# Linear attention on one core: one subtraction over both halves of a level's exponents, and an exponential for each half

## The chip, the cores and the metric

The kernel runs on one core of a Trainium2 chip. The metric is the device time in microseconds (us) of one execution. The core has five engines that run beside each other, each through its own list of instructions in order: PE (TensorE, matrix products), DVE (VectorE), ACT (ScalarE), POOL (GpSimd) and SP (SyncE, which issues most transfers). They wait for one another by semaphores.

## The reference, cut to what matters

The program is one inference step of a hybrid encoder. The part that is changed is gated linear attention, branch C: four heads, keys and values of 96 channels, with a decay that differs by channel and step.

```
def step(S, inp):
    qc, kc, vc, ac = inp
    b = jnp.cumsum(ac, axis=1)
    o_inter = jnp.einsum('blhk,bhkv->blhv', qc * jnp.exp(b), S)
    rel = b[:, :, None] - b[:, None, :]
    decay = jnp.exp(jnp.where(causal, rel, -jnp.inf))
    att = jnp.einsum('bthk,bshk,btshk->bhts', qc, kc, decay)
    o_intra = jnp.einsum('bhts,bshv->bthv', att, vc)
    bL = b[:, -1]
    S_new = jnp.exp(bL)[..., None] * S + jnp.einsum('bshk,bshv->bhkv', kc * jnp.exp(bL[:, None] - b), vc)
    return S_new, o_inter + o_intra
```

There are 512 prompt tokens and 8 x 16 sample tokens. Around this stand the input projections, stick-breaking attention (branch A), a pooling mixer (branch B), the gates and projections of the three branches, cross-attention and a feed-forward layer.

## The kernel before, in words

Tokens are worked in five tiles of 128: four of the prompt (0 to 3) and one of the samples (4), in the order 0, 1, 4, 2, 3. `gla_prep(i)` makes, for a tile, the transposed queries and keys (`qT`, `kT`), the log decays `la` (L721) and their running sums `bT` (matmul `pb`, L725, then ACT copies it, L728), and `E`, `kd` and `eL`. `gla_main(i)` computes the 128x128 attention of each head by levels of halving: at a level `hh` (64, 32, 16, 8, 4, 2, 1; for samples 8, 4, 2, 1) the tile is cut into blocks of 2*hh tokens, and the queries of a block's second half meet the keys of its first half. Both are scaled by the exponential of their distance from a reference, the running sum at the last token of the first half. `X`, a tile of 96x512 with two buffers, holds the scaled keys in each block's first half and the scaled queries in its second half. Four matmuls `pl` (L779) multiply them, and a predicated copy (L782) puts the result into `attT`.

So a level of hh > 1 is a chain over the engines: two subtractions on DVE (L771, L772), one exponential on ACT (L773), two products on DVE (L774 with the keys, L775 with the queries), `pl` on PE, the copy on DVE. There are 27 such levels (4 x 6 + 3), and five of hh = 1, which subtract only for the queries (L767, L768). The row forms in the trace tell the level: `pl` is 64, 96, 112, 120, 124, 126 or 127 rows high for hh = 64 to 1.

No order is written out by hand in this stage. A scheduler lists each engine's instructions when the program is built, and takes what is later in the program when what is earlier isn't ready by its own estimate. So PE's list here weaves the small matmuls of linear attention with the big ones of `branch` A, which comes next in the program: units of 24 matmuls `ps_g` (a gate) and 9 matmuls `ps_b` (a projection), each 128x320. This text calls them fill. A unit's gate is read by ACT (L875, the first of three exponential and logarithm steps with L877, L878; DVE clamps between, L876), and its projection by DVE (L883, into `mrg`). `ps_g` and `ps_b` share two PSUM buffers (tag "g"), so the next `ps_g` can start only when an earlier `ps_g` was read at L875 or an earlier `ps_b` at L883. The four units of the first 256 columns carry the weights `ga0` and `ba` in their names, the last four `ga3`.

Of the kernel before, what the change touches and what calls it, by code (L numbers as in the profile page):

```python
# [12 lines left out]
AF = mybir.ActivationFunctionType  # L13
ALU = mybir.AluOpType
# [14 lines left out]
TAU = 16.0  # L29
# [4 lines left out]
def tile_hybrid_stream_step(  # L34
# [9 lines left out]
    nc = tc.nc  # L44
# [18 lines left out]
    def bank(shape, tag="z", name="ps"):  # L63
        bufs = {"g": 2, "t": 2, "z": 2, "o": 2}[tag]
        return psum.tile(shape, F32, tag=tag, bufs=bufs, name=name)
# [243 lines left out]
    for hh in (64, 32, 16, 8, 4, 2, 1):  # L309
        nb = 64 // hh  # L310
# [433 lines left out]
    def gla_main(i, pre, S):  # L744
# [12 lines left out]
        for hh in levels:  # L757
            nb = 64 // hh
            nk = P - hh
            X = glw.tile([96, 4, P], F32, tag="X", bufs=2, name="X")  # L760

            def vw(t):
                return t.rearrange("p h (n two c) -> p (h n) two c", two=2, c=hh)
            bv, xv, kv, qv = vw(bT), vw(X), vw(kT), vw(qT)
            ref = bv[:, :, 0, hh - 1:hh].broadcast_to([96, 4 * nb, hh])
            if hh == 1:
                nc.vector.tensor_tensor(xv[:, :, 1, :], bv[:, :, 1, :], ref, ALU.subtract)  # L767
                nc.scalar.activation(xv[:, :, 1, :], xv[:, :, 1, :], AF.Exp, scale=1.0 / TAU)  # L768
                nc.gpsimd.tensor_copy(xv[:, :, 0, :], kv[:, :, 0, :])
            else:  # L770
                nc.vector.tensor_tensor(xv[:, :, 0, :], ref, bv[:, :, 0, :], ALU.subtract)  # L771
                nc.vector.tensor_tensor(xv[:, :, 1, :], bv[:, :, 1, :], ref, ALU.subtract)  # L772
                nc.scalar.activation(X, X, AF.Exp, scale=1.0 / TAU)  # L773
                nc.vector.tensor_tensor(xv[:, :, 0, :], xv[:, :, 0, :], kv[:, :, 0, :], ALU.mult)  # L774
            nc.vector.tensor_tensor(xv[:, :, 1, :], xv[:, :, 1, :], qv[:, :, 1, :], ALU.mult)  # L775
            pl = bank([P, 4, nb, hh], "z", "pl")
            for h in range(4):
                mv_ = X[:, h, :].rearrange("p (n two c) -> p n two c", two=2, c=hh)[:, :, 1, :]
                nc.tensor.matmul(pl[0:nk, h], X[:, h, 0:nk], mv_, start=True, stop=True)  # L779
            av = attT.rearrange("p h (n two c) -> p h n two c", two=2, c=hh)[0:nk, :, :, 1, :]  # L780
            mk = lmask[hh][0:nk, None, :, None].broadcast_to([nk, 4, nb, hh]).bitcast(U32)
            nc.vector.copy_predicated(av, mk, pl[0:nk])  # L782
# [71 lines left out]
    for j, i in enumerate(order):  # L854
        nxt = gla_prep(order[j + 1]) if j + 1 < NT else None
        if i == 4:
            gla_main(i, pre, None)
        else:
            S = gla_main(i, pre, S)
        pre = nxt  # L860
# [51 lines left out]
    X = resid.tile([P, NT, D], F32, name="X")  # L912
# [687 lines left out]
```

## Time and profile before

| what | value |
|---|---|
| time, median of 3 runs | 1289.25 us (1288.69 to 1289.4) |
| time of the profiled execution | 1288.69 us |
| its span, first to last instruction | 1287.0 us |
| outside the span | 1.69 us |
| mean granted TensorE clock | 0.995 |
| busy: PE, DVE, ACT, POOL | 1254.8, 778.7, 592.1, 43.3 us |

Busy time is the sum of an engine's instructions. What is left of the span for PE, 32.2 us, is the time in which it had nothing to run.

### The profile page before, as it was taken

How to read it: one execution, taken by the hardware profiler on the slowest of the kernel's cores; microseconds unless marked ns; L12 is line 12 of the kernel's file. 1: busy time of each engine (PE TensorE's matmuls, PEld its weight loads, DVE VectorE, ACT ScalarE, POOL GpSimd, SP SyncE). 2: the span in 40 equal slices, each digit the busy share in tenths (PEclk: the TensorE clock that was granted, in tenths of full speed). 3: DMA queues.
4: the chain of work that ended last, by engine and by line, in shares of the span. 5: the costliest groups of instructions: out<-in, count | busy, mean ns of one | idle time of the engine just before them, and what ended most of it. 6: DMA issues, size and time to landing. Idle time of an engine off the chain costs nothing.

```text
span 1287.0 us, 21345 instructions
## 1 busy us (share of the span) xinstructions
PE 1254.8 (98%) x8493; PEld 1151.8 (89%) x8493; DVE 778.7 (61%) x1456; ACT 592.1 (46%) x1200; POOL 43.3 (3%) x162
## 2 busy tenths in 40 slices
PE   8998989999999999999999999999999999999997
PEld 8997768988999999987998888889898989899996
DVE  7332767487478555537535544598466767675667
ACT  5323666555353445435444443475352525243353
POOL 2100121001000000000000000000000000000000
PEclk9999999999999999999999999999999999999999
DMA  7324232101321232231348960243132313132233
GB/s 241 102 79 132 86 100 62 53 15 56 83 65 46 83 96 72 95 131 66 121 160 299 324 227 1 82 148 95 54 107 72 100 50 114 50 99 83 83 109 121
DMA packets 132889, 133.88 MB, mean 104 GB/s; under 512 B 15798, under 2 KB 116741, under 8 KB 132789
## 3 DMA queue, kind: packets, MB, share of 16 engines
q1 hardware_dynamic: 132501, 132.23, 32.8%
q8 instruction: 67, 1.10, 0.4%
q0 software_dynamic: 288, 0.29, 0.1%
q14 instruction: 33, 0.27, 0.1%
HBM read 121.72 MB, written 10.77 MB: 103 GB/s over the span
## 4 chain that ended last, share of the span: by engine, by line
PE 88%; DVE 5%; ACT 2%; issue 2%; DMA 2%; POOL 0%; SPq 0%; DVEq 0%; ACTq 0%; POOLq 0%
PE ps_g L114 13%; PE fX L1351 11%; PE ps_d L114 8%; PE fZ L1351 5%; PE ps_n L114 5%; PE ps_b L114 4%; PE ps_xq L114 4%; PE acc L1423 4%; PE acc L1422 4%; PE acc L1424 4%; PE fY L1351 3%; PE ps_qk L114 3%; PE pl L779 2%; PE ps_xv L114 2%; PE ps_xk L114 2%
## 5 line engine op out<-in xcount | busy, mean ns | idle before, releaser
L1422 PE MATMUL acc<-wh_o,ga_h 128*128 128x512 f32 (+1 forms) x224 | 87.3, 390 | 0.0
L1423 PE MATMUL acc<-wl_o,ga_h 128*128 128x512 f32 (+1 forms) x224 | 87.2, 389 | 0.0
L1424 PE MATMUL acc<-wh_o,ga_l 128*128 128x512 f32 (+1 forms) x224 | 87.2, 389 | 0.0
L875 ACT ACTIVATE sgm<-ps_g 128x320 f32<-128x320 f32 x48 | 20.9, 436 | 65.6 <-PE ps_g L114 65.5
L1424 PEld LDWEIGHTS acc<-wh_o,ga_l 128*128 128x128 f32 x224 | 42.0, 188 | 9.6
L1422 PEld LDWEIGHTS acc<-wh_o,ga_h 128*128 128x128 f32 x224 | 42.0, 188 | 9.2
L1423 PEld LDWEIGHTS acc<-wl_o,ga_h 128*128 128x128 f32 x224 | 42.1, 188 | 9.2
L1351 PE MATMUL fX<-fT_h,wl_f 128*128 128x320 f32 x160 | 49.5, 309 | 0.0
L1351 PE MATMUL fX<-fT_l,wh_f 128*128 128x320 f32 x160 | 49.4, 309 | 0.0
L1351 PE MATMUL fZ<-S_h,wl_f 128*128 128x320 f32 x160 | 49.4, 309 | 0.0
L1351 PE MATMUL fX<-fT_h,wh_f 128*128 128x320 f32 x160 | 49.4, 309 | 0.0
L1351 PE MATMUL fX<-S_h,wh_f 128*128 128x320 f32 x160 | 49.4, 309 | 0.0
L1351 PE MATMUL fX<-S_l,wh_f 128*128 128x320 f32 x160 | 49.4, 309 | 0.0
L1351 PE MATMUL fZ<-S_l,wh_f 128*128 128x320 f32 x160 | 49.4, 308 | 0.0
L1351 PE MATMUL fZ<-S_h,wh_f 128*128 128x320 f32 x160 | 49.4, 308 | 0.0
L1351 PE MATMUL fX<-S_h,wl_f 128*128 128x320 f32 x160 | 49.3, 308 | 0.0
L143 ACT CAST wh_f<-ra 128x1024 fp32r<-128x1024 f32 x20 | 21.0, 1052 | 46.3 <-PE acc L1424 27.1
L144 DVE TENSOR_TENSOR wl_f<-ta,wh_f 128x1024 fp32r<-128x1024 f32 x20 | 24.5, 1226 | 27.5 <-ACT wh_f L143 27.5
L876 DVE TENSOR_SCALAR sgm<-sgm 128x320 f32<-128x320 f32 x48 | 15.5, 325 | 40.4 <-ACT sgm L875 40.3
L143 ACT CAST wh_f<-ta 128x1024 fp32r<-128x1024 f32 x20 | 21.0, 1049 | 38.9 <-PE acc L1424 29.0
L144 DVE TENSOR_TENSOR wl_f<-ra,wh_f 128x1024 fp32r<-128x1024 f32 x20 | 24.5, 1223 | 23.8 <-ACT wh_f L143 23.6
L1507 DVE TENSOR_TENSOR X<-acc,X 128x512 f32<-128x512 f32 x40 | 27.2, 690 | 18.1 <-PE acc L1424 18.1
(1001 smaller groups left out, 4218.2 us busy)
## 6 DMA issues: line engine op xcount, KB each, us to landing
raw_o<-in_w_ffn_out_dram SPq DMA_DIRECT2D x22, 512.0 KB, 3.5
ra<-in_w_ffn_in_dram SPq DMA_DIRECT2D x40, 256.0 KB, 3.3
rb<-in_w_ffn_in_dram SPq DMA_DIRECT2D x40, 256.0 KB, 3.3
kc<-in_cache_mem_k_dram SPq DMA_DIRECT2D x16, 512.0 KB, 5.1
vc<-in_cache_mem_v_dram SPq DMA_DIRECT2D x16, 512.0 KB, 5.5
raw_mix<-in_w_mix_out_dram SPq DMA_DIRECT2D x8, 512.0 KB, 4.2
raw_xo<-in_w_xo_dram SPq DMA_DIRECT2D x8, 512.0 KB, 4.6
kn<-in_cache_sb_k_dram SPq DMA_DIRECT2D x24, 128.0 KB, 2.5
```

What stands on the lines that cost most here:

```text
L114: ins = nc.tensor.matmul(ps, a, b, start=(j == 0), stop=(j == len(todo) - 1))
L143: nc.scalar.copy(h, src)
L144: nc.vector.tensor_tensor(l, src, h.bitcast(F32), ALU.subtract)
L779: nc.tensor.matmul(pl[0:nk, h], X[:, h, 0:nk], mv_, start=True, stop=True)
L875: nc.scalar.activation(s, ps, AF.Exp, scale=-1.0)
L876: nc.vector.tensor_scalar(s, s, 2.0 ** 63, None, ALU.min)
L1351: nc.tensor.matmul(ps, w_, m_, start=(start and j == 0), stop=(stop and j == 11), skip_group_check=True)
L1422: nc.tensor.matmul(ps, ah, wh[:, 0, c0:c0 + w], start=first, stop=False)
L1423: nc.tensor.matmul(ps, ah, wl[:, 0, c0:c0 + w], start=False, stop=False)
L1424: nc.tensor.matmul(ps, al, wh[:, 0, c0:c0 + w], start=False, stop=last)
L1507: nc.vector.tensor_tensor(dst, ps, dst, addop)
```

## The change

One subtraction over the whole of `X` takes the reference from both halves, so both halves hold b - ref. The first half needs ref - b, so its sign is wrong, and the exponential is done for each half by itself with the scales -1/TAU and +1/TAU. Nothing else is edited. The lines after L773 move down by one in the changed kernel: L774 and L775 are L775 and L776 there, L779 is L780, L782 is L783, L883 is L884.

```diff
             else:
-                nc.vector.tensor_tensor(xv[:, :, 0, :], ref, bv[:, :, 0, :], ALU.subtract)
-                nc.vector.tensor_tensor(xv[:, :, 1, :], bv[:, :, 1, :], ref, ALU.subtract)
-                nc.scalar.activation(X, X, AF.Exp, scale=1.0 / TAU)
+                both = bv[:, :, 0:1, hh - 1:hh].broadcast_to([96, 4 * nb, 2, hh])
+                nc.vector.tensor_tensor(xv, bv, both, ALU.subtract)
+                for r_ in range(2):
+                    nc.scalar.activation(xv[:, :, r_, :], xv[:, :, r_, :], AF.Exp, scale=(-1.0, 1.0)[r_] / TAU)
                 nc.vector.tensor_tensor(xv[:, :, 0, :], xv[:, :, 0, :], kv[:, :, 0, :], ALU.mult)
             nc.vector.tensor_tensor(xv[:, :, 1, :], xv[:, :, 1, :], qv[:, :, 1, :], ALU.mult)
```

The scheduler lists the instructions of this stage anew. Three places show it.

PE, from the state product `pk` of tile 1 through the levels of the sample tile 4, and the preparation of tile 3 (`pb`, `pd`, `tp_q`, `tp_k`, `tp_lr`). Before:

```order
L822 MATMUL pk<-vg_nat,qk_nat 96x96 x4
L755 MATMUL pa<-qT,kT 128x128
L779 MATMUL pl<-X 120x64 x4
L114 MATMUL ps_b<-oa_h,wl_ba_3844 128x320
L114 MATMUL ps_g<-hT_h,wh_ga0a 128x320
...
L779 MATMUL pl<-X 124x64 x4
L114 MATMUL ps_g<-hT_h,wl_ga0b 128x320
...
L725 MATMUL pb<-tri,la 96x128 x4
```

In the list before, 25 fill matmuls stand between `pk` and `pb`: one and 14 around the first level's end, 10 behind the second. Changed:

```order
L823 MATMUL pk<-vg_nat,qk_nat 96x96 x4
L780 MATMUL pl<-X 120x64 x4
L780 MATMUL pl<-X 124x64 x4
L725 MATMUL pb<-tri,la 96x128 x4
L732 MATMUL pd<-la,suf 128x384
L780 MATMUL pl<-X 126x64 x4
L780 MATMUL pl<-X 127x64 x4
L703 MATMUL tp_q<-ident,qk_nat 96x128 x4
L707 MATMUL tp_k<-ident,qk_nat 96x128 x4
L755 MATMUL pa<-qT,kT 128x128
L711 MATMUL tp_lr<-ident,lr_nat 16x128
```

All fill is gone from between them: those 25, and 13 more that stood between `pb` and the last `pa`. The next `ps_g` comes six rows further down.

DVE at the same place, from the update of the state `S` with `pk` to the log decays `la` that `pb` multiplies, and on to the products into `mrg` that free the fill's buffers. Changed (before, one L883 stood ahead of tile 1's last L782, and the second four rows behind L721):

```order
L829 SCALAR_TENSOR_TENSOR S<-S,eL,pk 96x96 x4
...
L772 TENSOR_TENSOR X<-bT 96x512
...
L845 TENSOR_TENSOR vg_nat<-po_g,t 128x384
L721 SCALAR_TENSOR_TENSOR la<-z_g,la 128x384
L847 TENSOR_TENSOR vg_nat<-vg_nat,qk_nat 128x384
L776 TENSOR_TENSOR X<-X,qT 96x128x2
L776 TENSOR_TENSOR X<-X,qT 96x256
L884 TENSOR_TENSOR mrg<-ps_b,sgm 128x320 x2
```

Two reads of `ps_b`, which before stood apart and earlier, stand together behind the sample tile's last two levels. Both "g" buffers hold a `ps_b` until then.

PE at the last levels of tile 2, changed (before, 14 fill matmuls stood between levels 124 and 126, and 8 between 126 and 127):

```order
L114 MATMUL ps_b<-oa_h,wl_ba_4390 128x320
L780 MATMUL pl<-X 124x64 x4
L899 MATMUL tp_oc<-ident,vg_nat 128x128 x5
L780 MATMUL pl<-X 126x64 x4
L780 MATMUL pl<-X 127x64 x4
L755 MATMUL pa<-qT,kT 128x128 x4
```

Five small transposes (`tp_oc`) are left between level 124 and level 126, and nothing between 126 and 127.

## Rows read from the trace of the kernel before

**Rows 1.** The page, part 1: busy time of each engine.

```profile
PE 1254.8 (98%) x8493; PEld 1151.8 (89%) x8493; DVE 778.7 (61%) x1456; ACT 592.1 (46%) x1200; POOL 43.3 (3%) x162
```

**Rows 2.** Busy time in stretches: engines, then PE clock, DMA share, GB/s.

```profile
core 0: us, PE busy (x) PEld busy (x) DVE busy (x) ACT busy (x) POOL busy (x), PEclk, DMA share, GB/s
240.00:420.00 180.00, 176.09 (x1301) 162.83 (x1300) 125.60 (x328) 86.32 (x178) 8.69 (x25) 1.00 0.19 53
420.00:1280.00 860.00, 856.32 (x5455) 788.66 (x5453) 519.55 (x880) 385.79 (x756) 0.21 (x1) 1.00 0.35 113
```

**Rows 3.** Timeline of PE from 236 to 425 us, its rows with idle time.

```profile
282.64 0.97 PE L779 MATMUL pl<-X 96*112 96x64 f32 x8 [0.57 <-DVE X L775]
289.69 0.42 PE L114 MATMUL ps_b<-oa_h,wh_ba 128*128 128x320 f32 x1 [0.53 <-ACT sgm L875]
368.51 0.65 PE L779 MATMUL pl<-X 96*64 96x64 f32 x8 [0.15 <-DVE X L775]
376.82 0.41 PE L114 MATMUL ps_b<-oa_h,wh_ba 128*128 128x320 f32 x1 [0.53 <-ACT sgm L875]
400.23 0.97 PE L779 MATMUL pl<-X 96*112 96x64 f32 x8 [1.53 <-DVE X L775]
407.75 1.95 PE L779 MATMUL pl<-X 96*126 96x64 f32 x16 [0.39 <-DVE X L775]
```

**Rows 4.** Groups by form: busy us, mean ns, idle ahead and its releaser.

```profile
L771 DVE TENSOR_TENSOR X<-bT 96x256 f32<-96x256 f32 x27 | 11.2, 415 | 1.0 <-PE pk L807 0.5 <-ACT bT L728 0.5
L772 DVE TENSOR_TENSOR X<-bT 96x256 f32<-96x256 f32 x27 | 11.1, 412 | 0.0
L773 ACT ACTIVATE X<-X 96x512 f32<-96x512 f32 x27 | 16.9, 627 | 20.9 <-DVE X L772 20.9
L741 DVE TENSOR_TENSOR E<-E,qT 96x512 f32<-96x512 f32 x5 | 3.4, 683 | 0.8 <-POOL eL L738 0.7
```

**Rows 5.** Timeline of DVE: start, duration, instruction; one after another.

```profile
280.67 0.69 DVE L741 TENSOR_TENSOR E<-E,qT 96x512 f32<-96x512 f32 x1 [0.67 <-POOL eL L738]
281.27 0.55 DVE L735 TENSOR_TENSOR qk_nat<-qk_nat 128x384 f32<-128x384 f32 x1
...
284.65 0.41 DVE L771 TENSOR_TENSOR X<-bT 96x256 f32<-96x256 f32 x1
284.99 0.41 DVE L772 TENSOR_TENSOR X<-bT 96x256 f32<-96x256 f32 x1
```

**Rows 6.** Timeline of ACT, instructions one after another.

```profile
282.86 0.63 ACT L773 ACTIVATE X<-X 96x512 f32<-96x512 f32 x1 [0.48 <-DVE X L772]
283.40 0.51 ACT L835 ACTIVATE qk_nat<-qk_nat 128x384 f32<-128x384 f32 x1
...
290.00 0.45 ACT L768 ACTIVATE X<-X 96x256 f32<-96x256 f32 x1
290.33 0.47 ACT L877 ACTIVATE sgm<-sgm 128x320 f32<-128x320 f32 x1
```

**Rows 7.** Timeline of PE from `pk` of tile 1 to `pb`.

```profile
296.64 0.84 PE L822 MATMUL pk<-vg_nat,qk_nat 128*96 128x96 f32 x8
297.32 0.41 PE L755 MATMUL pa<-qT,kT 96*128 96x128 f32 x2
297.57 0.95 PE L779 MATMUL pl<-X 96*120 96x64 f32 x8
298.33 0.40 PE L114 MATMUL ps_b<-oa_h,wl_ba 128*128 128x320 f32 x1
298.56 0.31 PE L114 MATMUL ps_g<-hT_h,wh_ga0a 128*128 128x320 f32 x1
298.71 0.32 PE L114 MATMUL ps_g<-hT_l,wh_ga0a 128*128 128x320 f32 x1
...
303.05 1.11 PE L725 MATMUL pb<-tri,la 128*96 128x128 f32 x8
```

**Rows 8.** Timeline of DVE over the same stretch.

```profile
297.52 0.98 DVE L828 SCALAR_TENSOR_TENSOR S<-S,eL,pk 96x96 f32<-96x96 f32 x4 [0.37 <-PE pk L822]
298.42 0.54 DVE L842 TENSOR_REDUCE ss<-sq 128x4 f32<-128x384 f32 x1
298.89 0.68 DVE L756 TENSOR_TENSOR attT<-pa,ident 128x512 f32<-128x512 f32 x1
...
299.96 0.42 DVE L782 COPY_PREDICATED attT<-lm,pl 120x256 f32<-120x256 uint32 x1
300.29 0.15 DVE L160 TENSOR_TENSOR t<-t,m 128x4 f32<-128x4 f32 x1
300.36 0.41 DVE L771 TENSOR_TENSOR X<-bT 96x256 f32<-96x256 f32 x1
...
301.98 0.55 DVE L844 TENSOR_TENSOR vg_nat<-po_g,t 128x384 f32<-128x384 f32 x1
302.45 0.55 DVE L721 SCALAR_TENSOR_TENSOR la<-z_g,la 128x384 f32<-128x384 f32 x1
```

## The prediction

> **What bounds the kernel now.** The page's busy times come first: PE is busy for 98% of the span, DVE for 61%, ACT for 46% [rows 1]. So the time is PE's work plus PE's idle time, and an edit on DVE and ACT can move the time only through what PE waits for. The table of stretches then says where that could be. The edited levels run between 240 and 420 us; in these 180 us PE is idle for 3.9 us, and in the 860 us behind for 3.7, at a granted clock of 1.00 in both [rows 2]. The idle time in the edited stretch is spread over six waits that the timeline of PE marks, 3.70 us in all [rows 3]. Two are for the exponential of a gate that a projection's buffer needs (0.53 each), four for `X` (0.57, 0.15, 1.53, 0.39). That is also the ceiling: if every wait went, the kernel would gain 3.7 us and no more. There is no such floor on a loss, because PE is kept busy there by fill that stands in its list between the levels, and the list changes.
>
> **The work itself.** Per level, two subtractions of 415 and 412 ns on DVE [rows 4] become one over 512 elements. What counts for a queue is start to start: 0.34 us for a 256-element subtraction, 0.60 for the 512-element product L741 [rows 5]. The new subtraction isn't in the trace; it lies between 0.60 and 2 x 0.34 = 0.68, and I take 0.60, because L741 has its width and engine. DVE gains 0.08 us a level, 2 us over 27 levels. On ACT one exponential of 512 takes 0.54 from start to start, one of 256 (L768) takes 0.33 [rows 6], so two take 0.66: 0.12 more a level, 3.2 us in all. Neither total is on PE's path, since DVE idles for 30% of the stretch and ACT for 52% [rows 2]; without that cover the pair would cost 3.2 - 2 = 1.2 us.
>
> The chain of one level gets shorter. Before, it is 0.34 + 0.41 for the subtractions, 0.63 for the exponential, 0.34 + 0.41 for the products: 2.13 us. Now the product with the keys needs only the first exponential: 0.68, then 0.45, then 0.34 + 0.41 with the second exponential under the first product: 1.88. A lone level is ready 0.25 us earlier, which is small beside what the lists do.
>
> The Trainium skill has a rule that speaks against the split ("ScalarE: Activation LUTs", section "What ACT_TABLE_LOAD costs"): an activation with immediate scale and bias takes 186 ns plus 0.833 ns an element, of which neighbours overlap by 93 ns. By it the split costs 93 ns a level, 2.5 us on ACT, where the rows give 3.2; its 612 ns for 512 elements stands beside 627 here. Were ACT the bound, the sum would be 0.5 us worse than nothing by the page, and 1.2 by the rows.
>
> **What the moved rows cost.** Three terms, each from a place shown with the change.
>
> (A) Behind `pk` of tile 1, PE has now two levels and nothing else before `pb`. `pb` waits for `la` from DVE, and DVE lists this ahead of it. With `pk`'s start as zero, the state's update starts at 0.88 (296.64 to 297.52) and takes 0.90 [rows 7, 8]. Then the reduction 0.47, two predicated copies of 0.33, the wide subtraction 0.60, the subtraction L767 and one product at 0.34 each, four small ones of 0.07, L844's product 0.47 [rows 5, 8]: 0.88 + 0.90 + 0.47 + 0.66 + 0.60 + 0.68 + 0.28 + 0.47 = 4.94. From the start of L721 to `pb` are 0.60 (302.45 to 303.05), so `pb` starts at 5.54. PE has `pk` for 0.68 and two levels of 0.76 [rows 7], 2.20 in all. It idles for 3.3 us. Before, 25 fill matmuls at 0.15 covered this, and they were there to be had: in the new list both shared buffers hold a `ps_b` that L884 frees behind `la`. Behind `pb`, `tp_lr` needs `qT` copied by ACT, the fifth of a row of ACT steps of about 0.5 with two DVE products in it, while PE has some 3.5 us of work: I put 0.3, an estimate between 0 and 0.6. A = 3.6.
>
> (B) At the end of tile 2, levels 124, 126 and 127 stand with no fill. Count from the start of 124's product with the queries. DVE then has 0.34 for it, 0.60 for the subtraction, 0.47 for a gate product, 0.33 for a copy, 0.34 for the product with the keys; the product with the queries starts at 2.08 and ends at 2.5. PE starts level 124 at 0.45, takes 0.76, and five small transposes take it to about 1.8: it waits 0.7. Level 126 ends for DVE about 1.0 behind its start, at 3.5; a copy and one product more make level 127 ready at 4.25, and PE, free at 3.3, waits 0.95. Together 1.65; I take 1.5, because PE may come a little late to 124. The bounds are 0.8 (one of the two waits) and 2.2.
>
> (C) The waits of before. At both 1.53 and 0.57 the list now has fill between a level's product and its matmul, or DVE's rows ahead are fewer, so they go: -2.1. The two waits for a gate's exponential stay in number: four units there now take the buffer of their own gate, and in two of them a level stands between. The waits of 0.15 and 0.39 grow by 0.3 together, since at these places the wide casts stand ahead of the subtraction. Fewer changes between small and big matmuls (46 where 50 were, counted in the two lists) save 0.08 each (0.23 for 0.15 from start to start [rows 7]): -0.3.
>
> Sum: +3.6 + 1.5 - 2.1 + 0.3 - 0.3 = +3.0 us. Against the profiled execution (1288.69, span 1287.0 and 1.69 outside) that is 1291.7. The median of the runs, 1289.25, is 0.56 above that execution; on it the sum gives **1292.2 us**. Nothing behind 420 us gives the delay back, because PE idles for only 3.7 us in 860 there [rows 2] and the transfers are released by the same engines.
>
> **The rivals.**
>
> 1. *The gaps are half filled: about the same.* DVE and ACT run ahead of my count at A, because some rows counted there come early, or the sample levels don't wait. For it: DVE idles there before, 0.37 us ahead of the state's update alone [rows 8]. Against: the update needs `pk`, and all else is behind it. With A at 1.8 and B at 0.8 the sum is +0.5: 1289.8.
>
> 2. *The shorter chain wins: faster.* If A and B cost nothing, what stays is -2.1 - 0.3, and with the two gate waits hidden behind levels another -1.06; the sum is -2.4 to -3.5: 1286.3 in the middle. The point that decides is whether `la` is ready 3.3 us earlier than I count. For it is the 0.25 us a level, against it a DVE list of 4 us behind `pk`. A measurement can tell 0.2%, 2.6 us, from no change, so only the lower half of this counts as faster.
>
> 3. *The exponentials pile up: slower still.* ACT's 0.12 a level comes on the path where levels stand bare (seven of them: 0.8 us), and all four units that take their own gate's buffer wait 0.53, two more than before: +1.9 on top of the forecast, 1294.1. For it are the two waits of this kind in [rows 3]; against it, ACT idles for half of the stretch [rows 2].
>
> 4. *The new subtraction isn't one pass at full rate*, as its reference repeats over both halves. At 0.68 it adds 0.08 at each bare level, 0.5 us: 1292.7. L771 reads the same repeated reference at full rate [rows 5].
>
> **How the numbers follow.** Forecast with rival 4: 0.45; rival 1: 0.33; rival 2: 0.12; rival 3: 0.10. The bound of slower is 1291.83, just under the forecast. Of the forecast and rival 4 some three quarters lie above it, all of rival 3: 0.34 + 0.10, and a little of rival 1's upper edge: slower 0.48. Faster, under 1286.67: 0.08. The same: 0.44. The forecast alone runs from 1290.5 to 1294. The range of 8 in 10 reaches from 1287.0, within rival 2, to 1295.0, above rival 3.
>
> **What would show it.** In the profile of the changed kernel: one row of about 680 ns for the subtraction (27 times) and 54 exponentials of about 440; a wait of about 3 us of PE at `pb` of tile 3, released by DVE at L721, with no `ps_g` between; waits at levels 126 and 127 of tile 2; no wait of 1.5 us at a level 112; PE's busy time in the stretch as before, and its idle time near 7 us instead of 3.9. The prediction is wrong if PE's wait at that `pb` is under 1.5 us, or if the time behind the stretch differs by more than 1 us.

## The result and the profile after

The changed kernel takes 1297.92 us (median of 4 runs, 1296.53 to 1298.7), the kernel before 1289.33 beside it (4 runs, 1288.69 to 1291.23). The ratio is 1.0053, with a 95% interval of 1.003 to 1.0075: slower. The two medians are 8.6 us apart; the ratio stands for 6.8 us and its interval for 3.9 to 9.7. Forecast was +3.0. The profiled execution has a span of 1295.4 us after 1287.0, so 8.4 us are to be found in it (0.4 of them ahead of the stage: the first `pb`, of tile 0, starts at 237.55 us before and at 237.99 after). Its mean granted TensorE clock is 0.989; it was 0.995.

The page's busy times of the changed kernel, which answer to [rows 1], show little:

```profile
PE 1260.8 (97%) x8493; PEld 1157.4 (89%) x8493; DVE 777.5 (60%) x1429; ACT 596.3 (46%) x1227; POOL 41.7 (3%) x162
```

DVE has 1.2 us less and ACT 4.2 more. But PE, with the same 8493 matmuls, is busy for 6.0 us longer. Since the number of matmuls is the same and their time isn't, the next view to read is the clock. The two stretches of [rows 2], after the change:

```profile
240.00:420.00 180.00, 172.51 (x1246) 158.90 (x1245) 122.07 (x296) 86.10 (x199) 7.14 (x25) 0.97 0.20 54
420.00:1280.00 860.00, 857.07 (x5469) 790.50 (x5468) 514.12 (x867) 386.60 (x751) 0.21 (x1) 1.00 0.35 112
```

In the edited stretch PE now idles for 7.5 us (3.9 before), and its clock, which stood at 1.00, is 0.97 in the mean. Behind it nothing has changed. The waits of PE in the stretch, which answer to [rows 3] (of its timeline the rows with idle time; those between are left out here too):

```profile
301.65 1.77 PE L725 MATMUL pb<-tri,la 128*96 128x128 f32 x8 [3.27 <-DVE la L721]
344.10 0.53 PE L802 MATMUL po_g<-st,qp 96*32 96x96 f32 x8 [0.20 <-DMA st<-in_state_gla_dram]
364.99 0.41 PE L114 MATMUL ps_g<-hT_h,wh_ga3a 128*128 128x320 f32 x1 [0.42 <-ACT sgm L876]
370.78 0.41 PE L114 MATMUL ps_b<-oa_h,wh_ba 128*128 128x320 f32 x1 [0.53 <-ACT sgm L876]
383.31 1.06 PE L780 MATMUL pl<-X 96*126 96x64 f32 x8 [0.75 <-DVE X L776]
385.52 1.07 PE L780 MATMUL pl<-X 96*127 96x64 f32 x8 [1.16 <-DVE X L776]
398.75 0.42 PE L114 MATMUL ps_b<-oa_h,wh_ba 128*128 128x320 f32 x1 [0.53 <-ACT sgm L876]
407.05 1.06 PE L780 MATMUL pl<-X 96*126 96x64 f32 x8 [0.52 <-DVE X L776]
```

They add up to 7.38 us; before it was 3.70. The first is the place that the prediction calls A, the fifth and sixth are its B. (It names the `pb` of A as tile 3's. It is tile 2's; what stands right behind it is the preparation of tile 3.) The two waits of 1.53 and 0.57 at a level 112 are gone. So the extra idle time is 3.7 us, less than half of the 8.4.

Note the duration in the first row: `pb` takes 1.77 us, where it took 1.11 before [rows 7]. Cut into single microseconds around that row, and into pairs around the sixth, PE reads (busy time, granted clock, DMA share, GB/s):

```profile
301.00:302.00 1.00, 0.35 (x3) 0.98 0.00 0
302.00:303.00 1.00, 1.00 (x7) 0.50 0.00 0
...
304.00:305.00 1.00, 1.00 (x5) 0.50 0.00 0
305.00:306.00 1.00, 1.00 (x10) 0.82 0.00 0
...
384.00:386.00 2.00, 0.84 (x9) 1.00 0.00 0
386.00:388.00 2.00, 2.00 (x17) 0.82 0.03 8
388.00:390.00 2.00, 2.00 (x11) 0.50 0.01 4
...
392.00:394.00 2.00, 2.00 (x13) 0.50 0.00 0
394.00:396.00 2.00, 2.00 (x15) 0.97 0.00 0
```

Right behind A and right behind B the granted clock is 0.50, that is 1.2 GHz in place of 2.4. Half of the time spent there, taken as lost, gives an estimate of the price: at A 0.02 + 3 x 0.5 + 0.18 = 1.7 us, at B 2 x 0.18 + 6 x 0.5 + 2 x 0.03 = 3.4 us, 5.1 in all. With 3.7 of idle time that is 8.8, where the stage has lost 8.0. The estimate at B is too high, as a run below shows; the fewer changes between small and big matmuls, which the prediction put at -0.3, are not seen by themselves.

The edited instructions are as forecast. Groups by form, in the columns of [rows 4]:

```profile
L772 DVE TENSOR_TENSOR X<-bT 96x512 f32<-96x512 f32 x27 | 18.3, 682 | 1.2 <-PE pl L780 0.8 <-ACT bT L728 0.5
L774 ACT ACTIVATE X<-X 96x256 f32<-96x256 f32 x54 | 19.7, 415 | 12.3 <-DVE X L772 11.1 <-DVE t L160 0.9
```

The wide subtraction takes 682 ns, as L741 of the same width takes 683 [rows 4].

### The profile page after: what moved, and what is told of

The parts are those of the page before. It is cut to its first block, busy times and chain, and to the rows that moved or that the text cites. A ratio compares the mean times of both kernels' runs of the same rounds, so it can differ in the third digit from the quotient of the medians.

```text
span 1295.4 us, 21340 instructions
## 1 busy us (share of the span) xinstructions
PE 1260.8 (97%) x8493; PEld 1157.4 (89%) x8493; DVE 777.5 (60%) x1429; ACT 596.3 (46%) x1227; POOL 41.7 (3%) x162
## 4 chain that ended last, share of the span: by engine, by line
PE 87%; DVE 5%; issue 2%; ACT 2%; DMA 2%; POOL 0%; SPq 0%; DVEq 0%; ACTq 0%; POOLq 0%
PE ps_g L114 13%; PE fX L1352 11%; PE ps_d L114 8%; PE fZ L1352 5%; PE ps_n L114 5%; PE ps_xq L114 4%; PE ps_b L114 4%; PE acc L1424 4%; PE acc L1423 4%; PE acc L1425 4%; PE fY L1352 3%; PE ps_qk L114 3%; PE pl L780 2%; PE ps_xk L114 2%; PE ps_xv L114 2%
```

## The experiments

Two theories. **L**: the loss lies in the lists. The scheduler lists the stage anew, two places of PE's list are left bare of fill, PE idles there, and its clock falls behind them. **W**: the loss lies in the work of the changed levels, above all the second exponential. A rival within L, called **C**: the fall of the clock costs nothing of its own.

### Work and lists apart

The lists of all engines are held by an edge of order alone, without a semaphore, from each instruction to the one ahead of it in a table of numbers (the table itself says nothing to a reader). At the end of the program:

```diff
+    for names in lists.values():
+        for a, b in zip(names, names[1:]):
+            tc.add_manual_dep(ins[f"I-{b}"], f"I-{a}", mybir.DependencyInfo(
+                mybir.DependencyClass.NoSync, mybir.DependencyReason.DATA), reason="pin")
```

`new_work_old_lists` is the changed kernel in the order of before: the wide subtraction stands where the second of the two stood, the two exponentials where the one did. Expected:

> The changed computation (one wide subtraction, two exponentials), with every engine's list held in the order that it had before the change. Theory L (the loss is the new order of the lists: 3.7 us more idle time of PE, and 5.1 us in which TensorE runs at 1.2 GHz behind two of these waits): no wait of over 2 us, granted clock 1.00 from 240 to 420 us, and 1289.3 us, the time before, within 1 us; if the chain that is 0.25 us shorter shortens the old wait of 1.53 us at a level 112, down to 1288.5. Rival W (the loss is the work: ACT has 3.2 us more, and each level's second exponential comes late): the loss stays, 1296 to 1298.

Measured: 1290.92 us (12 runs), ratio 1.001, interval 0.9996 to 1.0024. In its profile the clock is back at 1.00. The stretch, for PE alone (length, busy time, clock, DMA share, GB/s):

```profile
240.00:420.00 180.00, 176.11 (x1302) 1.00 0.19 53
```

The waits are nearly those of [rows 3], 3.72 us in all; two of them from PE's timeline:

```profile
281.95 1.00 PE L780 MATMUL pl<-X 96*112 96x64 f32 x8 [0.49 <-DVE X L776]
...
399.51 0.97 PE L780 MATMUL pl<-X 96*112 96x64 f32 x8 [1.53 <-DVE X L776]
```

The loss is gone with the list, as L has it. The wait of 1.53 us did not move by a hundredth, though the chain of a level is shorter. (DVE's own rows fill the time ahead of it: a copy of the level before at 397.34, held until PE was done with that level, then L845, a product, L847 and the product L776 at 398.95, without a pause.)

`old_work_new_lists` is the kernel before in the order of after. Expected:

> The computation of before (two subtractions, one exponential), with every engine's list held in the order that it has after the change. Theory L: PE waits about 3.3 us at pb of tile 2 and twice at the last levels of tile 2, the granted clock falls to 0.50 behind both places, and the time is that of the changed kernel, 1297 to 1299 us (the longer chain of a level may add some tenths at the two bare levels). Rival W: 1289 to 1290.5.

Measured: 1300.15 us (6 runs), ratio 1.0085 (1.0065 to 1.0105). The old computation has the whole loss, at the same two places (the second and third row of PE's timeline are B):

```profile
301.02 2.02 PE L725 MATMUL pb<-tri,la 128*96 128x128 f32 x8 [3.73 <-DVE la L721]
382.91 1.06 PE L779 MATMUL pl<-X 96*126 96x64 f32 x8 [0.84 <-DVE X L775]
385.12 1.94 PE L779 MATMUL pl<-X 96*127 96x64 f32 x8 [1.16 <-DVE X L775]
```

Two of PE's stretches behind these places:

```profile
302.00:304.00 2.00, 2.00 (x7) 0.50 0.00 0
...
386.00:388.00 2.00, 2.00 (x10) 0.50 0.03 8
```

It is 1 us over what was expected, as the wait at `pb` is 0.46 us longer than in the changed kernel and the stretch has a mean clock of 0.95, where that has 0.97. W falls: the work of the change without its list costs nothing that can be measured (0.24% or 3 us at the most, by the interval), and the list without the work costs all of it.

### The clock apart from the idle time

In `fill_both_gaps`, `fill_first_gap` and `fill_second_gap` the changed kernel keeps its own lists, held in the same way, and PE gets matmuls that nobody reads. They are written into the bank that the real matmul then overwrites:

```diff
         pb = bank([96, 4, P], "t", "pb")
+        for _ in range(13 if i == 2 else 0):
+            nc.tensor.matmul(pb[:, 0, :], ident[:, 0:96], tri, start=True, stop=True)
...
             pl = bank([P, 4, nb, hh], "z", "pl")
+            for _ in range({2: 3, 1: 5}.get(hh, 0) if i == 2 else 0):
+                nc.tensor.matmul(pl.rearrange("p h n c -> p (h n c)")[:, 0:P], ident, ident, start=True, stop=True)
```

Both places:

> The changed kernel with its lists held, and matmuls whose result is never read in front of three matmuls that PE waits for: 13 ahead of pb of tile 2 (13 x 0.23 = 3.0 us of the 3.27), 3 ahead of level 126 and 5 ahead of level 127 of tile 2 (0.7 and 1.1 us). They do nothing for the work; pb and the levels still start when DVE is done. Theory L with the clock as its larger part: the granted clock stays at 1.00 through both places and 5.1 us come back (1.7 behind the first, 3.4 behind the second): 1297.9 - 5.1 = 1292.8 us, which is the forecast's sum. Rival C (the fall of the clock costs nothing of its own, because PE waits for DVE and ACT there anyway): 1297.9, or more, as the added matmuls can only delay.

Measured: 1292.36 us (11 runs), ratio 1.0021 (1.0008 to 1.0033). Against 1297.92 that is 5.6 us less, for 21 matmuls more. PE's timeline at A:

```profile
296.77 3.03 PE L725 MATMUL pb<-tri,ident 128*96 128x128 f32 x26
300.23 1.11 PE L727 MATMUL pb<-tri,la 128*96 128x128 f32 x8 [0.43 <-DVE la L721]
```

And PE in stretches around A and B:

```profile
298.00:304.00 6.00, 5.57 (x48) 1.00 0.01 4
380.00:392.00 12.00, 12.00 (x102) 1.00 0.00 1
```

The first row of the timeline is the unread work. From `pk`'s start to the real `pb` are 5.82 us (294.41 to 300.23), in the changed kernel 5.80 (295.85 to 301.65): `pb` comes no earlier, and only the clock is different. At B it is the same: from level 126 to level 127 are 2.26 us here and 2.21 in the changed kernel. C falls: all 11 executions here (up to 1295.18 us) are shorter than all 4 of the changed kernel (from 1296.53), and 1292.36 lies at the forecast of 1292.2, which had no term for the clock.

The same matmuls stand behind both places in the two kernels, so the price of the clock can be read from row to row. Here:

```profile
303.54 0.60 PE L703 MATMUL tp_q<-ident,qk_nat 128*96 128x128 f32 x4
...
382.73 1.07 PE L785 MATMUL pl<-X 96*127 96x64 f32 x8
...
390.48 0.81 PE L785 MATMUL pl<-X 96*96 96x64 f32 x8
```

In the changed kernel:

```profile
306.64 0.60 PE L703 MATMUL tp_q<-ident,qk_nat 128*96 128x128 f32 x4
...
396.32 0.81 PE L780 MATMUL pl<-X 96*96 96x64 f32 x8
```

From `pb` to `tp_q` are 3.31 us here and 4.99 there, from level 127 to the next tile's level 96 7.75 and 10.80 (385.52 to 396.32). So the clock cost 1.7 us behind A and 3.05 behind B, 4.7 together. With the 3.7 of idle time that is 8.4, where the stage has lost 8.0. By the medians the price is 5.6 us, by the ratios (1.0053 and 1.0021) 4.1. No run holds the changed kernel's lists without the added matmuls, so what the holding itself does to the time is not shown apart.

The first place alone:

> The same with only the 13 matmuls ahead of pb of tile 2. Theory L: the clock falls only behind the last levels of tile 2, and 1.7 us come back: 1296.2 us. Rival C: 1297.9.

Measured: 1296.31 us (6 runs), ratio 1.0051 (1.0033 to 1.0069). By the medians 1.6 us are back, as forecast; by the ratios it is 0.3, so this time alone doesn't show the first place's price. `fill_both_gaps`, measured beside it, is 3.95 us faster, which is the second place's. The second place alone:

> The changed kernel with its lists held and unread matmuls at the second place only: 3 ahead of level 126 and 5 ahead of level 127 of tile 2. Theory L with the clock: the wait at pb of tile 2 stays at 3.3 us and the clock falls behind it, but not behind level 127, and 3.4 us come back: 1297.9 - 3.4 = 1294.5 us. With the first place's 1.6 us this adds up to the 5.5 us that filling both gave. Rival C (clock without effect): 1297.9.

Measured: 1294.38 us (12 runs), ratio 1.0028 (1.0008 to 1.0048): 3.5 us back by the medians, 3.2 by the ratios. The two add up to 5.1 by the medians and 3.5 by the ratios, beside 5.6 and 4.1 for both together. An interval is 4 to 5 us wide, so the second place's price is well shown by the times, and the first place's rests on the rows above.

### Each half of the edit, lists free

`two_subs_two_exps` splits the exponential only:

```diff
-                nc.scalar.activation(X, X, AF.Exp, scale=1.0 / TAU)
+                for r_ in range(2):
+                    nc.scalar.activation(xv[:, :, r_, :], xv[:, :, r_, :], AF.Exp, scale=1.0 / TAU)
```

> One part of the change alone: an exponential for each half, but the two subtractions of before; lists free. The list that comes of it leaves levels 112, 120, 124, 126 and 127 of tile 1 bare (one after the other with only a small transpose and one matmul between), and 126 and 127 of tile 2; pb of tile 2 has 13 fill matmuls ahead. Theory L: waits of about 1 us at each bare level (some 5 us in tile 1, 1.5 in tile 2), the clock at 0.50 behind both, none at pb of tile 2: 1296 to 1301 us. Rival W (the second exponential costs at each level): no such grouping, 27 small delays, and about 1291 (27 x 0.12 us over before).

Measured: 1305.81 us (5 runs), ratio 1.0119 (1.0101 to 1.0136), more than expected of either theory. In PE's timeline the bare levels of tile 1 are where they were expected, and the third row is a wait that was not (`pb` of tile 3):

```profile
286.65 1.46 PE L780 MATMUL pl<-X 96*124 96x64 f32 x8 [1.27 <-DVE X L776]
289.38 1.93 PE L780 MATMUL pl<-X 96*126 96x64 f32 x8 [1.27 <-DVE X L776]
382.45 1.83 PE L725 MATMUL pb<-tri,la 128*96 128x128 f32 x8 [1.50 <-DVE la L721]
```

PE in stretches behind the bare levels:

```profile
288.00:292.00 4.00, 2.29 (x11) 0.50 0.00 0
...
296.00:300.00 4.00, 4.00 (x21) 0.50 0.00 0
300.00:304.00 4.00, 4.00 (x23) 0.50 0.00 0
```

Its eleven waits are 8.3 us, 4.6 more than before, and the mean clock of the stretch is 0.93: 0.07 x 180 = 12.6 us. Together that is 17.2, near the 16.5 measured. So the half of the edit that gives ACT 3.2 us more to do comes with a list that loses 16. (Its list was not run with the old work; that the loss is the list's rests here on these waits and the clock.)

`one_sub_one_exp` makes one wide subtraction and one exponential:

```diff
-                nc.vector.tensor_tensor(xv[:, :, 0, :], ref, bv[:, :, 0, :], ALU.subtract)
-                nc.vector.tensor_tensor(xv[:, :, 1, :], bv[:, :, 1, :], ref, ALU.subtract)
+                nc.vector.tensor_tensor(xv, bv, both, ALU.subtract)
```

> The other part alone: one wide subtraction and one exponential over both halves. It leaves out the sign of the first half (exp of b - ref in place of ref - b), so its time alone is of use. Its list has fill at pb of tile 2 (3 ps_g and a ps_b) and at the end of tile 2; bare are 126 of the sample tile's end and 120 of the sample tile's start, not longer than in the kernel before. Theory L: 1288 to 1291 us, clock 1.00. Rival W2 (a wide subtraction that is late for both halves costs): 1292 or more with waits at the levels.

Measured: 1288.08 us (12 runs), ratio 0.9988 (0.9976 to 1.0001). Its list leaves 2.21 us of waits, and the clock stays at 1.00. W2 falls.

### A list with fill, from the code

`new_work_frees_fill` asks for one thing: that the product which frees a fill's buffer is listed as early as it can run, so that the next unit of fill is there for the bare places.

```diff
                     if mode == "first":
-                        nc.vector.tensor_tensor(m, pb, s, ALU.mult)
+                        with tc.high_priority():
+                            nc.vector.tensor_tensor(m, pb, s, ALU.mult)
                         continue
```

> The changed kernel with one more edit, no list held: the product L884 that reads a unit's ps_b and frees its buffer is listed with high priority, as early as its inputs allow. In the lists that come of it 16 fill matmuls stand again between pk of tile 1 and pb of tile 2, and 13 between levels 126 and 127 of tile 2; bare are only level 127 of tile 1 and level 126 of tile 2. Theory L (the loss is bare places in PE's list, and the clock behind them): no wait over 1.5 us, granted clock 1.00 from 240 to 420 us, 1287 to 1290 us. Rival W (the loss is the work of the changed levels): 1296 to 1298 as before this edit.

Measured: 1287.19 us (12 runs), ratio 0.9987 (0.9972 to 1.0003). That is 10.7 us under the changed kernel by the medians and 8.5 by the ratios, with one line of code. PE's waits in the stretch are 2.52 us; these are the three longest:

```profile
305.46 1.07 PE L780 MATMUL pl<-X 96*127 96x64 f32 x8 [0.43 <-DVE X L776]
393.76 0.41 PE L114 MATMUL ps_b<-ob_h,wh_bb 128*128 128x320 f32 x1 [0.71 <-DVE mrg L885]
396.30 0.42 PE L114 MATMUL ps_g<-hT_h,wl_gb0b 128*128 128x320 f32 x1 [0.68 <-DVE wl_gb0b L89]
```

The stretch as a whole, for PE:

```profile
240.00:420.00 180.00, 177.34 (x1315) 1.00 0.19 52
```

The same kernel was measured once more:

> The changed kernel with L884 at high priority once more, since its interval of 0.9972 to 1.0003 leaves open whether it is faster than the kernel before. If the list is what counts, with 1.2 us less waiting of PE in the stage than before (2.5 us where 3.7 were): 1286.5 to 1288.5 us, a ratio of 0.998 to 0.9995. If the first measurement was chance: 1289 to 1290.

Measured: 1287.7 us (12 runs) beside 1290.49 for before, ratio 0.9977 (0.996 to 0.9994): faster than the kernel before in this measurement by 0.2%, in the first by 0.1% with an interval that holds no change.

`old_work_frees_fill` is that line in the kernel before:

> The same edit on the kernel before: L883 with high priority. Its list has fill at the three places that the prediction spoke of, and single bare levels (112 of tile 2, 120 of tile 3). Theory L: as before within 1.5 us, 1287.5 to 1290.5, and within 1 us of the changed kernel with the same edit. If the new work is worth something by itself (DVE 2 us less, a chain 0.25 us shorter), it shows here as a difference between the two.

Measured: 1289.12 us (12 runs), ratio 1.0001 (0.9982 to 1.002). The profiled execution took 1296.87 us, the second longest of these 12. PE's waits in it are 2.11 us, less than before, but the mean clock of the stretch is 0.97. It is 1.00 up to the wait below, and 0.50 from 408 to 416 us, behind it:

```profile
406.01 0.42 PE L114 MATMUL ps_g<-hT_h,wh_gb0a 128*128 128x320 f32 x1 [1.27 <-DVE sgm L886]
```

So fewer idle microseconds are no promise of a steady clock. By the medians old and new work with this line are 1.9 us apart, where at most 1 was expected, but the intervals overlap. Whether the change itself is worth a microsecond stays open.

All kernels side by side: the sum of PE's waits from 240 to 420 us and the mean clock of that stretch in the profiled execution, and the median time.

| kernel | waits, us | clock | time, us |
|---|---|---|---|
| before | 3.70 | 1.00 | 1289.33 |
| changed | 7.38 | 0.97 | 1297.92 |
| `new_work_old_lists` | 3.72 | 1.00 | 1290.92 |
| `old_work_new_lists` | 7.87 | 0.95 | 1300.15 |
| `fill_first_gap` | 4.32 | 0.97 | 1296.31 |
| `fill_second_gap` | 5.26 | 0.97 | 1294.38 |
| `fill_both_gaps` | 2.42 | 1.00 | 1292.36 |
| `two_subs_two_exps` | 8.27 | 0.93 | 1305.81 |
| `one_sub_one_exp` | 2.21 | 1.00 | 1288.08 |
| `new_work_frees_fill` | 2.52 | 1.00 | 1287.19 |
| `new_work_frees_fill`, second time | 2.54 | 0.98 | 1287.7 |
| `old_work_frees_fill` | 2.11 | 0.97 | 1289.12 |

Unread matmuls count as busy, so the three kernels with them have that much less waiting without being the faster for it. The profile is one execution and the time a median over several with different clocks: the profiled execution lies up to 2.4 us from the median, and that of `old_work_frees_fill` 7.8 us above it. The medians of the kernel before, taken anew beside each group of runs, go from 1288.89 to 1290.49, so times of different groups are good to 1 or 2 us.

## Why the prediction was right and wrong

**The step that failed is the price of an idle microsecond.** The prediction adds the waits of A and B at their own length, beside a clock that it read as 1.00 in the stretch [rows 2], and asks nowhere what PE's clock does behind a wait. A clock of 1.00 is that of before's waits in this stage, of which the longest is 1.53 us [rows 3]. Behind the new ones it fell, and the runs with unread matmuls show that this cost about 5 us (5.6 by the medians, 4.7 by the rows, 4.1 by the ratios), more than the 3.7 by which the waits grew. The same step stands in the prediction's first paragraph, where the time is PE's work plus its idle time and the work is taken as fixed: PE was busy for 6.0 us longer with the same 8493 matmuls. Neither of its two signs of being wrong came, because both look at waits and at the time behind the stretch. The warning was in the trace, in another stage. PE of the kernel before, by stretch (busy time, clock, DMA share, GB/s):

```profile
120.00:124.00 4.00, 1.61 (x8) 0.87 0.84 230
124.00:128.00 4.00, 2.97 (x4) 0.50 0.51 145
128.00:132.00 4.00, 4.00 (x15) 0.50 0.00 0
...
176.00:180.00 4.00, 1.54 (x13) 1.00 0.73 208
```

The first stretch has PE idle for more than half of its time, and the next two stand at 0.50. The Trainium skill has the rule, on its page "TensorE: Matmul & The Clock Gate", section "Part 1: The HAM clock gate (the "warmup" mystery)": the array runs at 2.4 GHz only while it is kept busy, and idling takes it back to 1.2 GHz. The trace agrees at A (0.50 behind 3.27 us without a matmul). It also shows that the length of a wait alone doesn't tell: the last row has PE idle for 2.46 us at a clock of 1.00, while behind the 0.75 and 1.16 of B it fell to 0.50.

**A was right.** Counted were 5.54 us from `pk` to `pb` and a wait of 3.3; measured are 5.80 and 3.27, released by DVE at L721, with no `ps_g` between (`pb` came 0.26 later than counted and PE's own work ahead of it took 0.3 longer; that the two cancel in the wait is luck). The 0.3 for `tp_lr` did not come.

**B was right in place and near in size.** Counted were 0.7 and 0.95, taken as 1.5; measured are 0.75 and 1.16, which is 1.91, inside the bounds of 0.8 to 2.2.

**C was half right.** The 2.1 us came back: no wait at a level 112. The two waits of 0.53 for a gate's exponential stayed in number. The 0.15 went and the 0.39 became 0.52, so the 0.3 put on them did not come. Not foreseen are 0.42 at a `ps_g` behind such an exponential and 0.20 at a transfer. All waits together grew by 3.7 us, where the terms held 3.3.

**The rest.** Work of the levels: as counted, and hidden, as `new_work_old_lists` shows. Two exponentials take 0.73 us together (the row below, of the changed kernel), one took 0.63 [rows 4]; 27 times 0.1 us found room on ACT. Nothing behind 420 us gave anything back, as forecast: from the first `ps_xq` that waits to the end of the span are 655.1 us before (631.90 to 1287.0) and 654.9 after (640.47 to 1295.4).

```profile
285.80 0.73 ACT L774 ACTIVATE X<-X 96x256 f32<-96x256 f32 x2
```

**The rivals.** 1 (gaps half filled) and 2 (the shorter chain wins) fell with A and B at full size. 2 stands on a chain of one level, and at the wait of 1.53 us that chain turned out not to be what PE waits for: with the chain 0.25 us shorter and the list the same, the wait is the same. DVE's rows ahead set it. 3 (exponentials pile up) gave a time nearest to the truth, 1294.1, but for a cause that the lists held apart refute: that is luck. 4 fell by 682 against 683 ns, and 0.60 us from start to start (298.53 to 299.13 in DVE's timeline). None of them held the clock, so the range ended at 1295.0.

## What to carry to other kernels

Where a scheduler orders the instructions, an edit's price is mostly that of the list that it makes. Read the new list for places where PE has no independent work, and hold the old list to price the edit alone: here the work was worth 0.1% with no certain sign, while lists that lost, lost 0.5% to 1.2%. Price a new wait of PE with the clock behind it, from a stretch of the same trace in which PE idled, and not by its length alone: waits that grew by 3.7 us cost 8.4. Where fill is missing, look for what holds its buffers; one product listed earlier gave back all of the loss.

## What the runs showed of the hardware that was not expected

- The same wait does not always take the clock down, and not for the same time. Behind B the stretch of 370 to 420 us has a mean clock of 0.93 in the changed kernel and 0.90 in `fill_first_gap`, whose waits there are the same 0.75 and 1.16 us. In the second measurement of `new_work_frees_fill` the clock fell where no wait was over 0.44 us, with the samples' last level, `z_g`, `pa` and `po_g` following one another; in the first, at the same place, it did not:

```profile
306.00:308.00 2.00, 1.56 (x13) 1.00 0.01 4
308.00:310.00 2.00, 2.00 (x12) 0.96 0.24 44
310.00:312.00 2.00, 2.00 (x11) 0.50 0.65 218
312.00:314.00 2.00, 2.00 (x11) 0.69 0.00 0
```

- A PE that the profile shows as busy need not get its clock back at once. In `two_subs_two_exps` it is busy for 4.00 of 4 us in each stretch from 292 to 304 us, with the end of tile 1 and the beginning of the sample tile, and its clock stays at 0.50. It rises again behind the first fill, which begins at 303.25.
- The granted clock goes with much of the scatter. Of 77 executions of the kernel before that ran beside these experiments, the 34 with a mean clock of 0.995 or more have a median of 1288.5 us (1286.7 to 1290.9), the 11 with 0.990 or less one of 1293.9 (1290.8 to 1298.3).
